# Slots of whole 256-byte lines, and pools that begin at 0 modulo 256, in a two-layer decoder kernel

## The chip, the cores and the metric

The kernel runs on one core of a Trainium2 chip. The metric is the device time of one execution in microseconds (us), as the median of several runs. On-chip memory (SBUF) has 128 partitions; an address below is a byte address within a partition, the same in all 128. TensorE multiplies a stationary operand (the weights, loaded ahead of each product) with a moving operand and adds into PSUM. VectorE, ScalarE and GpSimd work element by element, and SyncE issues most transfers.

## The reference

Two post-norm decoder layers on x (512 tokens x 1024), conditioned by a vector c. In outline, for each layer:

```
ada = silu(c) @ w_ada + b_ada                  # six rows: sh1 sc1 g1 sh2 sc2 g2
u   = layer_norm(x) * (1 + sc1) + sh1
proj = u @ w_in + b_in                         # 1024 -> 6660 columns
y_n = pooling, gated convolution, block-sparse attention, forgetting attention   # 256 wide each
merged = sum_n sigmoid(gate_n) * (y_n @ w_branch[n])
x = layer_norm(ALPHA * x + g1 * (merged @ w_o)) * ln1_g + ln1_b
u2 = layer_norm(x) * (1 + sc2) + sh2
hdn = square(relu(u2 @ w_up + b_up))           # 1024 -> 4096
x = layer_norm(ALPHA * x + g2 * (hdn @ w_down)) * ln2_g + ln2_b
```

All inputs and the output are float32.

## The kernel before

Every large product is made of three products on operands split in two: a value is rounded to the format `float32r` (the high part), and the remainder is the low part. `split` (L120 to L122) does this with one copy on ScalarE and one subtraction on VectorE; `mm3` (L126 to L129) multiplies high by high, high by low and low by high, which the trace shows as the lines L127, L128 and L129 (L85 where the first projection's order is written out by hand).

SBUF is given out by pools, one after another: `cp` (constants and small columns), `up` (25 slots of 4096 bytes called `unit`), `wp` (`uT`, and the weight buffers), `tp` (5 scratch slots called `t2`), `sp` (small columns). Within a pool, tiles of one tag share the tag's slots in turn, and a slot is as large as the largest tile of its tag. The tags of `wp` that matter here:

- `uT`, one tile: the modulated and transposed activations, 8 blocks k x (high, low) x 512 tokens, 32768 bytes.
- `whl`, 4 slots: split weights. Most tiles have 8192 bytes, as (high, low) x 8 x 128 or as 2 x 1024; `token_values` has tiles of 8 x 256 and, once in a layer, of 8 x 260 floats, 8320 bytes, which sets the size of the slots.
- `raw`, 2 slots: weights as they are loaded, with the same largest tile of 8320 bytes.
- `aw`, `rawb`, `whb`: 2048 bytes a slot.

A `t2` tile has at most 528 floats, 2112 bytes.

The work goes in stages: the first projection with its normalisation (order written by hand in `START`), `token_values`, the mixers' projections (`project`), the gates (`gates`), attention run between the tiles of other stages, the output projection (`out_project` on `w_o`), the up projection (`project` on `w_up`), and the down projection (`out_project` on `w_down`); then the second layer. In `project` a 1 MB piece of weights goes into `raw`, is split into two `whl` tiles of 128 columns, and each `whl` tile is the stationary operand of 8 k x 3 = 24 matmuls whose moving operand is a 512-token row of `uT` (for the first four tiles of two of the projections of a layer, the two 256-token halves apart). In `out_project` the activations in a `unit` slot are the stationary operand, and the weights in `whl` move: 4 token blocks x 2 halves x 3 = 24 matmuls for each k. The last k's there have their split weights in `unit` slots (`held`). In `gates`, `whl` is the stationary operand against `uT`, and `whb` against `unit`.

Waits between engines are put in by the framework from the tiles' use; the order on each engine is that of the program apart from what its planner moves.

Of the kernel before, what the change touches and what calls it, by code (L numbers as in the profile page):

```python
# [7 lines left out]
F32 = mybir.dt.float32  # L8
F32R = mybir.dt.float32r
BF16 = mybir.dt.bfloat16  # L10
# [6 lines left out]
P = 128  # L17
# [14 lines left out]
RAW_BUFS = 2  # L32
WHL_BUFS = 4
WHB_BUFS = 2
AW_BUFS = 2
T2_BUFS = 5
NH = 4
ATT_RATE = 1.1
ATT_RATE2 = 1.2
# [27 lines left out]
def decoder_kernel(ctx, tc, x, c, positions, w_ada, b_ada, w_in, b_in, w_pool, pool_scale, conv_w,  # L67
# [22 lines left out]
    cp = ctx.enter_context(tc.tile_pool(name="cp", bufs=1))  # L90
    up = ctx.enter_context(tc.tile_pool(name="up", bufs=UNITS))
    wp = ctx.enter_context(tc.tile_pool(name="wp", bufs=1))
    tp = ctx.enter_context(tc.tile_pool(name="tp", bufs=T2_BUFS))
    sp = ctx.enter_context(tc.tile_pool(name="sp", bufs=6))
    pp = ctx.enter_context(tc.tile_pool(name="pp", bufs=1, space=PSUM))

    cnt = [0]

    def nm(s):
        cnt[0] += 1  # L100
        return f"{s}_{cnt[0]}"

    def unit(shape=(P, 1024), dt=F32):
        return up.tile(list(shape), dt, tag="unit", name=nm("unit"))

    def t2(n=512, dt=F32):
        return tp.tile([P, n], dt, tag="t2", name=nm("t2"))

    def small(n=1, tag="s1"):
        return sp.tile([P, n], F32, tag=tag, name=nm("s"))  # L110
# [20 lines left out]
    def load(dst, src):  # L131

        ins = nc.sync.dma_start(dst, src)
        if ordered[0]:
            tc.keep_in_program_order(ins)
            ordered[1] = ins.ins.name
        else:
            tc.add_manual_dep(ins.ins, ordered[1], mybir.DependencyInfo(
                mybir.DependencyClass.NoSync, mybir.DependencyReason.DATA), reason="after the start")
        return ins  # L140
# [10 lines left out]
    c8 = cp.tile([KD, P], F32, name="c8")  # L151
    cst = cp.tile([P, NKEPT], F32, name="cst")
    cst2 = t2()[:, 0:NCONST - NKEPT]
    S.dma_start(c8, c[0].rearrange("(r p) -> r p", p=P))
    S.dma_start(cst, consts[:, 0:NKEPT])
    S.dma_start(cst2, consts[:, NKEPT:NCONST])
    posi = t2(dt=I32)
    G.dma_start(posi, positions.broadcast_to([P, T]))
    ident = cst[:, C_IDENT:C_IDENT + P]
# [16 lines left out]
    def mean_rstd(xt, sums):  # L176

        nmean, rstd = small(), small()
        if len(sums) == 2:
            V.tensor_scalar(nmean, sums[0], sums[1], -1.0 / D, op0=ALU.add, op1=ALU.mult)  # L180
        else:
            V.tensor_scalar(nmean, sums[0], -1.0 / D, None, op0=ALU.mult)
        S.activation(t2(1024, BF16), xt, AF.Square, bias=nmean, accum_out=rstd)  # L183
        return nmean, rstd
# [174 lines left out]
    def ada_flush():  # L359
        while pending:  # L360
            ada_step()
# [72 lines left out]
            split(uT[:, 4 * h:4 * h + 4, 0, i * P:(i + 1) * P], uT[:, 4 * h:4 * h + 4, 1, i * P:(i + 1) * P], v)  # L434


    def load_raw(shape, parts, tag="raw"):
        raw = wp.tile([P] + list(shape), F32, tag=tag, name=nm(tag), bufs=RAW_BUFS)
        for dst, src in parts:
            last_load[0] = load(dst(raw), src)  # L440
        return raw
# [1 line left out]
    last_load = [None]  # L443

    def whl(shape):
        return wp.tile([P] + list(shape), F32R, tag="whl", name=nm("whl"), bufs=WHL_BUFS)

    def kcols(w, c0, n):
        return w[:, c0:c0 + n].rearrange("(k p) m -> p k m", p=P)
# [1 line left out]
    def col_weights(w, c0, n=256):  # L451

        raw = load_raw((KD, n), [(lambda r: r, kcols(w, c0, n))])
        for j in range(n // P):
            t = whl((2, KD, P))
            split(t[:, 0], t[:, 1], raw[:, :, j * P:(j + 1) * P])
            yield t

    def project(w, tiles, evac, nh):

        heads = []
        for ci, c0 in enumerate(tiles):
            for j, t in enumerate(col_weights(w, c0)):
                idx = 2 * ci + j
                if idx < nh:
                    ps = bank("mm" if idx < PB["mm"] else "br")
                    for k in range(KD):
                        mm3(ps[:, 0:256], t[:, 0, k], t[:, 1, k], uT[:, k, 0, 0:256], uT[:, k, 1, 0:256],
                            k == 0, k == KD - 1)
                    heads.append((idx, ps, t))  # L470
                    if len(heads) == nh:
                        for i2, p2, tt in heads:
                            for k in range(KD):
                                mm3(p2[:, 256:512], tt[:, 0, k], tt[:, 1, k], uT[:, k, 0, 256:512],
                                    uT[:, k, 1, 256:512], k == 0, k == KD - 1)
                            evac(i2, p2)
                else:
                    ps = bank("mm")
                    for k in range(KD):
                        mm3(ps, t[:, 0, k], t[:, 1, k], uT[:, k, 0], uT[:, k, 1], k == 0, k == KD - 1)  # L480
                    evac(idx, ps)
                if idx >= nh + 1:
                    flush_stores()
                soon_step()
                ada_step(ada_rate[0])
                between_step(ATT_RATE)
# [4 lines left out]
    def token_values(l, c0, n):  # L491

        w = w_in[l]
        vb = sp.tile([P, 260], F32, tag="vb", name=nm("vb"), bufs=2)
        load(vb[:, :n], b_in[l:l + 1, c0:c0 + n].broadcast_to([P, n]))
        raw = load_raw((KD, n), [(lambda r: r, kcols(w, c0, n))])
        th, tl = whl((KD, n)), whl((KD, n))
        split(th, tl, raw)
        v2 = [unit((P, 2, 2, 4, 64), F32R) for _ in range(2)]
        z = None  # L500
        if n > 256:
            z = small(16, "z")
        for i in range(NT):
            ps = bank("mm")
            cs = slice(i * P, (i + 1) * P)
            for k in range(KD):
                mm3(ps[:, :n], uT[:, k, 0, cs], uT[:, k, 1, cs], th[:, k], tl[:, k], k == 0, k == KD - 1)
            vt = t2()
            V.tensor_tensor(vt[:, :n], ps[:, :n], vb[:, :n], op=ALU.add)
            v4 = vt[:, 0:256].rearrange("p (r h d) -> p r h d", r=2, h=2)  # L510
            dst = v2[i // 2][:, i % 2]
            split(dst[:, :, 0::3], dst[:, :, 1:3], v4)
            between_step(V_RATE)
            if z is not None:
                V.tensor_copy(z[:, 4 * i:4 * i + 4], vt[:, 256:260])
        return v2, z
# [192 lines left out]
    def out_project(w, grow, nk, n_outer, act, finish, g_row, b_row, xsrc):  # L709
# [13 lines left out]
        for k in range(nk):  # L723
            if k % 2 == 0:
                raw = load_raw((2, 1024), [(lambda r: r, w[k * P:(k + 2) * P, :].rearrange("(a p) m -> p a m", p=P))])
            if k < n_outer + HELD_WHL:
                t = whl((2, 1024))
                wh, wl = t[:, 0], t[:, 1]
            else:
                wh, wl = unit(dt=F32R), unit(dt=F32R)  # L730
            V.tensor_tensor(raw[:, k % 2], raw[:, k % 2], grow, op=ALU.mult)  # L731
            split(wh, wl, raw[:, k % 2])
            ah, al = act(k)
            if k < n_outer:
                for i in range(NT):
                    block(k, i, ah, al, wh, wl)
            else:
                held.append((k, ah, al, wh, wl))
            if k == nk - 2:
                with tc.issue_after(last_load[0].ins):  # L740
                    rows += [bcast(g_row), bcast(b_row)]
                    xts = [unit() for _ in range(NT)]
                    for i in range(NT):
                        load(xts[i], xsrc[i * P:(i + 1) * P, :])
# [144 lines left out]
    for l in range(DEPTH):  # L889
# [72 lines left out]
        else:  # L962
            project(w_in[l], [1024, 1280, 1792], first_evac, NH)
        wpool = [unit((P, 2, P)), unit((P, 2, 2, P), F32R)]
# [171 lines left out]
        ada_rate[0] = ADA_UP  # L1136
        project(w_up[l], list(range(0, FF, 256)), up_evac, NH)
        ada_flush()
# [68 lines left out]
```

## Time and profile before

| | us |
|---|---|
| median of 3 runs | 1622.05 |
| the 3 runs | 1623.7, 1620.67, 1622.05 |
| profiled execution, its own time | 1626.41 |
| its span, first to last instruction | 1624.6 |
| TensorE busy with matmuls | 1584.3 (98%) |
| VectorE busy | 994.4 (61%) |
| ScalarE busy | 740.4 (46%) |
[...]

The views are of the one profiled execution. [...]

### The profile page before, as it was taken

The numbers are of one execution on the slowest core, as the hardware profiler recorded it, in microseconds if no ns is written. First come the engines' busy times: TensorE is split into PE (matmuls) and PEld (weight loads), VectorE is DVE, ScalarE is ACT, GpSimd is POOL, SyncE is SP. The second block draws the span as 40 slices with busy tenths as digits, with TensorE's granted clock in tenths as the row PEclk, the third lists the DMA queues.
The fourth block names the chain that finished last, engine by engine and source line by source line (L and its number), as shares of the span: only waits on it lengthen the run. The fifth ranks groups of instructions, "written<-read, shape, count | busy, mean of one in ns | idle before, by whom it ended". The sixth has DMA issues, their size and how long they took to land.

```text
span 1624.6 us, 19880 instructions
## 1 busy us (share of the span) xinstructions
PE 1584.3 (98%) x7615; PEld 1309.9 (81%) x7615; DVE 994.4 (61%) x1641; ACT 740.4 (46%) x1230; POOL 54.8 (3%) x162
## 2 busy tenths in 40 slices
PE   5999999999999999999999999999999999999998
PEld 4878888888888888888898888778888988888886
DVE  6797455787674446744678845677467632275454
ACT  4565465443374435412365553645335543353131
POOL 1000000000010000000010000000001000000000
PEclk9999999999999999999999999999999999999999
DMA  9634223553636554332633422354216443223241
GB/s 317 185 97 154 94 88 98 168 157 117 225 101 191 187 153 134 104 104 80 244 110 120 127 75 91 117 158 153 88 62 234 147 124 95 87 104 104 79 181 52
DMA packets 151298, 215.54 MB, mean 133 GB/s; under 512 B 7564, under 2 KB 112991, under 8 KB 151203
## 3 DMA queue, kind: packets, MB, share of 16 engines
q1 hardware_dynamic: 148723, 206.84, 40.0%
q0 software_dynamic: 2176, 7.14, 1.2%
q8 instruction: 60, 0.98, 0.2%
q14 instruction: 35, 0.29, 0.1%
q10 hardware_dynamic: 304, 0.28, 0.1%
HBM read 205.33 MB, written 8.91 MB: 132 GB/s over the span
## 4 chain that ended last, share of the span: by engine, by line
PE 63%; issue 21%; DVE 8%; DMA 3%; ACT 3%; POOL 1%; SPq 1%; POOLq 0%; DVEq 0%; ACTq 0%
PE ps_mm L129 15%; PE ps_mm L127 14%; PE ps_mm L128 14%; PE ps_br L128 2%; PE ps_br L127 2%; PE ps_br L129 2%; PE ps_S L127 2%; PE ps_S L129 2%; PE ps_S L128 2%; PE ps_tr L129 2%; PE ps_tr L128 2%; PE ps_tr L127 2%; DMA aw<-in_w_ada_dram 1%; DVE whl L122 1%; DVE unit L122 1%
## 5 line engine op out<-in xcount | busy, mean ns | idle before, releaser
L127 PE MATMUL ps_mm<-uT,whl 128*128 128x512 f32 (+1 forms) x1280 | 491.6, 384 | 0.0
L129 PE MATMUL ps_mm<-uT,whl 128*128 128x512 f32 (+1 forms) x1280 | 488.7, 382 | 0.3 <-DVE whl L122 0.3
L128 PE MATMUL ps_mm<-uT,whl 128*128 128x512 f32 (+1 forms) x1280 | 487.4, 381 | 0.0
L122 DVE TENSOR_TENSOR whl<-raw,whl 128x1024 fp32r<-128x1024 f32 (+1 forms) x218 | 269.7, 1240 | 244.7 <-ACT whl L121 239.5
L121 ACT CAST whl<-raw 128x1024 fp32r<-128x1024 f32 (+1 forms) x218 | 230.0, 1059 | 193.6 <-PE ps_br L129 149.6
L129 PEld LDWEIGHTS ps_mm<-uT,whl 128*128 128x128 f32 x1280 | 241.6, 189 | 48.1 <-DVE whl L122 0.8
L128 PEld LDWEIGHTS ps_mm<-uT,whl 128*128 128x128 f32 x1280 | 241.8, 189 | 45.4
L127 PEld LDWEIGHTS ps_mm<-uT,whl 128*128 128x128 f32 x1280 | 241.7, 189 | 44.3
L317 DVE SCALAR_TENSOR_TENSOR unit<-aw,scol,unit 128x512 f32<-128x512 f32 x148 | 110.8, 748 | 99.2 <-DMA aw<-in_w_ada_dram 98.1
L1133 ACT ACTIVATE t<-ps_mm,cols 128x512 f32<-128x512 f32 x62 | 42.7, 689 | 185.8 <-PE ps_mm L129 185.8
L1078 ACT ACTIVATE t<-ps_mm,hgate 128x512 f32<-128x512 f32 x64 | 44.1, 690 | 181.3 <-PE ps_mm L129 181.1
L731 DVE TENSOR_TENSOR raw<-raw,unit 128x1024 f32<-128x1024 f32 x80 | 94.6, 1218 | 13.6 <-DMA raw<-in_w_down_dram 7.8
L1086 DVE SCALAR_TENSOR_TENSOR t<-t,ps_br 128x512 f32<-128x512 f32 x48 | 32.9, 686 | 83.9 <-PE ps_br L129 80.4
L127 PE MATMUL ps_mm<-whl,unit 128*128 128x512 f32 x180 | 70.7, 392 | 0.0
L129 PE MATMUL ps_mm<-whl,unit 128*128 128x512 f32 x180 | 70.7, 392 | 0.0
L128 PE MATMUL ps_mm<-whl,unit 128*128 128x512 f32 x180 | 70.5, 392 | 0.0
L121 ACT CAST unit<-unit 128x512 fp32r<-128x512 f32 (+1 forms) x94 | 54.5, 612 | 24.4 <-DVE unit L122 22.7
L122 DVE TENSOR_TENSOR unit<-unit,unit 128x512 fp32r<-128x512 f32 (+1 forms) x94 | 61.3, 678 | 5.8 <-ACT unit L121 5.5
L183 ACT ACTIVATE t<-unit,s 128x1024 bf16<-128x1024 f32 x28 | 32.1, 1148 | 57.0 <-DVE s L180 51.2
L188 POOL TENSOR_TENSOR s<-s,mhalf 128x1 f32<-128x1 f32 x30 | 17.2, 575 | 1026.7 <-DVE s L187 1022.1
L129 PE MATMUL ps_br<-unit,whb 128*128 128x512 f32 x128 | 50.0, 390 | 0.0
L127 PE MATMUL ps_br<-unit,whb 128*128 128x512 f32 x128 | 49.9, 390 | 0.0
(276 smaller groups left out, 2598.1 us busy)
## 6 DMA issues: line engine op xcount, KB each, us to landing
raw<-in_w_in_dram SPq DMA_DIRECT2D x47, 1024.0 KB, 5.4
aw<-in_w_ada_dram SPq DMA_DIRECT2D x160, 256.0 KB, 3.0
raw<-in_w_up_dram SPq DMA_DIRECT2D x32, 1024.0 KB, 6.0
raw<-in_w_down_dram SPq DMA_DIRECT2D x32, 1024.0 KB, 4.9
unit<-in_w_ada_dram SPq DMA_DIRECT2D x32, 256.0 KB, 5.7
rawb<-in_w_branch_dram SPq DMA_DIRECT2D x32, 256.0 KB, 3.1
raw<-in_w_o_dram SPq DMA_DIRECT2D x8, 1024.0 KB, 5.0
xmid<-unit POOLq DMA_DIRECT2D x12, 512.0 KB, 2.9
```

Of the source, the lines that this page charges most:

```text
L121: S.copy(hi, src)
L122: V.tensor_tensor(lo, src, rd(hi), op=ALU.subtract)
L127: TE.matmul(ps, wh, ah, start=first, stop=False)
L128: TE.matmul(ps, wh, al, start=False, stop=False)
L129: last_mm[0] = TE.matmul(ps, wl, ah, start=False, stop=last)
L183: S.activation(t2(1024, BF16), xt, AF.Square, bias=nmean, accum_out=rstd)
L188: G.tensor_tensor(rstd, rstd, mhalf, op=ALU.pow)
L317: V.scalar_tensor_tensor(a, aw, scol[:, k:k + 1], a, op0=ALU.mult, op1=ALU.add)
L731: V.tensor_tensor(raw[:, k % 2], raw[:, k % 2], grow, op=ALU.mult)
L1078: S.activation(tg, ps, AF.Tanh, bias=hgate[l][:, n * KD + d:n * KD + d + 1], scale=0.5)
L1086: V.scalar_tensor_tensor(tg, tg, 1.0, bp, op0=ALU.add, op1=ALU.mult)
L1133: S.activation(r, ps, AF.Relu, bias=cl[:, B_UP + idx:B_UP + idx + 1])
```

## The change

Three things about addresses, and nothing about what is computed or in which order it is written:

- `raw` and `whl` tiles are taken from a slot of `W_SLOT` = 2112 floats, 8448 bytes, which is 33 lines of 256 (before: 8320 bytes, 32.5 lines); `rawb`, which goes through the same function, from 512 floats, its size before. The function `slot` takes the whole slot and hands out its first part in the shape asked for.
- `t2` tiles are taken from slots of `T2_SLOT` = 2304 bytes, 9 lines (before: 2112 bytes, 8.25 lines).
- A tile of 40 floats, 160 bytes, that nothing reads or writes, is put first into the pool `cp`. The pools after it move up by these 160 bytes and then begin at 0 modulo 256.

```diff
+T2_SLOT = 2304
+W_SLOT = 2112
+CP_PAD = 40
...
     sp = ctx.enter_context(tc.tile_pool(name="sp", bufs=6))
+    cp.tile([P, CP_PAD], F32, name="pad")
...
     def t2(n=512, dt=F32):
-        return tp.tile([P, n], dt, tag="t2", name=nm("t2"))
+        bytes_ = 2 if dt == BF16 else 4
+        return tp.tile([P, T2_SLOT // bytes_], dt, tag="t2", name=nm("t2"))[:, 0:n]
...
+    def slot(shape, dt, tag, bufs):
+
+        n, size = 1, (W_SLOT if tag in ("raw", "whl") else 512)
+        for d in shape:
+            n *= d
+        t = wp.tile([P, size], dt, tag=tag, name=nm(tag), bufs=bufs)[:, 0:n]
+        if len(shape) == 2:
+            return t.rearrange("p (a b) -> p a b", b=shape[1])
+        return t.rearrange("p (a b c) -> p a b c", b=shape[1], c=shape[2])
+
     def load_raw(shape, parts, tag="raw"):
-        raw = wp.tile([P] + list(shape), F32, tag=tag, name=nm(tag), bufs=RAW_BUFS)
+        raw = slot(shape, F32, tag, RAW_BUFS)
...
     def whl(shape):
-        return wp.tile([P] + list(shape), F32R, tag="whl", name=nm("whl"), bufs=WHL_BUFS)
+        return slot(shape, F32R, "whl", WHL_BUFS)
```

## Rows read from the trace of the kernel before

**Rows 1.** The page: TensorE's busy time, and its granted clock in 40 slices.
```profile
PE 1584.3 (98%) x7615; PEld 1309.9 (81%) x7615; DVE 994.4 (61%) x1641; ACT 740.4 (46%) x1230; POOL 54.8 (3%) x162
...
PEclk9999999999999999999999999999999999999999
```

**Rows 2.** Busy time by stretch: us of the stretch, each engine, clock, DMA share, GB/s.
```profile
0.00:100.00 100.00, 77.26 (x386) 63.58 (x387) 78.91 (x169) 56.40 (x82) 9.48 (x25) 0.98 0.69 210
700.00:800.00 100.00, 100.00 (x437) 81.68 (x436) 47.33 (x44) 26.14 (x28) 0.00 (x0) 1.00 0.42 147
1000.00:1100.00 100.00, 95.65 (x468) 78.54 (x467) 66.27 (x140) 54.79 (x105) 2.63 (x14) 0.97 0.45 138
```

**Rows 3.** TensorE's waits: us in all, times, longest.
```profile
PE ps_tr L85 <- DVE unit L85: 7.3, 3, 4.1
...
PE ps_mm L129 <- DVE whl L122: 0.3, 1, 0.3
```

**Rows 4.** Matmuls by line and shape: count, busy us, mean ns of one.
```profile
L127 PE MATMUL ps_mm<-uT,whl 128*128 128x512 f32 x1136 | 450.8, 397 | 0.0
...
L127 PE MATMUL ps_mm<-whl,unit 128*128 128x512 f32 x180 | 70.7, 392 | 0.0
...
L127 PE MATMUL ps_tr<-whl,unit 128*128 128x512 f32 x120 | 47.1, 392 | 0.0
...
L127 PE MATMUL ps_S<-whl,unit 128*128 128x512 f32 x120 | 47.0, 392 | 0.0
...
L578 PE MATMUL ps_tr<-cst,t 128*128 128x128 f32 x160 | 28.5, 277 | 0.2
...
L127 PE MATMUL ps_mm<-uT,whl 128*128 128x256 f32 x144 | 40.9, 284 | 0.0
...
L127 PE MATMUL ps_br<-whl,unit 128*128 128x512 f32 x60 | 23.4, 390 | 0.0
```

**Rows 5.** Timeline, up projection: start us, length; every 24th start, two between.
```profile
594.73 0.40 PE L127 MATMUL ps_mm<-uT,whl 128*128 128x512 f32 x1
...
600.32 0.39 PE L127 MATMUL ps_mm<-uT,whl 128*128 128x512 f32 x1
...
601.46 0.39 PE L129 MATMUL ps_mm<-uT,whl 128*128 128x512 f32 x1
...
602.82 0.39 PE L129 MATMUL ps_mm<-uT,whl 128*128 128x512 f32 x1
...
605.78 0.40 PE L127 MATMUL ps_mm<-uT,whl 128*128 128x512 f32 x1
...
611.37 0.39 PE L127 MATMUL ps_mm<-uT,whl 128*128 128x512 f32 x1
```

**Rows 6.** Timeline, down projection: every 24th start.
```profile
673.18 0.40 PE L127 MATMUL ps_tr<-whl,unit 128*128 128x512 f32 x1
...
678.78 0.39 PE L127 MATMUL ps_tr<-whl,unit 128*128 128x512 f32 x1
...
684.23 0.40 PE L127 MATMUL ps_tr<-whl,unit 128*128 128x512 f32 x1
```

**Rows 7.** Timeline, up projection's 256-token halves: every 24th start.
```profile
479.24 0.28 PE L127 MATMUL ps_mm<-uT,whl 128*128 128x256 f32 x1
...
482.08 0.28 PE L127 MATMUL ps_mm<-uT,whl 128*128 128x256 f32 x1
...
484.96 0.28 PE L127 MATMUL ps_br<-uT,whl 128*128 128x256 f32 x1
```

**Rows 8.** Timeline, products of units with units: the first start and the 64th.
```profile
794.70 0.39 PE L127 MATMUL ps_tr<-unit,unit 128*128 128x512 f32 x1
...
808.98 0.39 PE L127 MATMUL ps_mm<-unit,unit 128*128 128x512 f32 x1
```

**Rows 9.** Timeline of VectorE, up projection: the subtractions of two successive tiles.
```profile
596.59 1.23 DVE L122 TENSOR_TENSOR whl<-raw,whl 128x1024 fp32r<-128x1024 f32 x1 [2.00 <-ACT whl L121]
...
603.90 1.22 DVE L122 TENSOR_TENSOR whl<-raw,whl 128x1024 fp32r<-128x1024 f32 x1
```

## The prediction, made before the kernel was run

> **What bounds the kernel now.** I read the page first: TensorE is busy for 1584.3 of 1624.6 us and its granted clock is in the top tenth in every slice [rows 1], so only its own pace can move the time much. The stretches say where that holds: in 700:800 it is busy all the time, at clock 1.00; it lacks 22.7 us in the first 100 us and 4.4 us in 1000:1100 [rows 2]. Its waits are short: the longest kind, on VectorE at the start, is 7.3 us in all, and the products of `uT` with `whl` (L129) wait 0.3 us in all for the splits that feed them [rows 3]. A wait that ended sooner is therefore worth next to nothing; the spacing of matmul starts is worth everything, since 4,848 products of 512 columns with a `whl` operand (3 x 1136, and 3 x 480) fill most of the span [rows 4]. "Busy" and the mean of one (397 ns) don't show this spacing, because a matmul's modelled span overlaps the next one's; I took it from the starts in the timeline.
>
> That is where this case is decided. In the up projection each `whl` tile gives 24 matmuls (8 k x 3 terms), and every 24th start is listed: tiles last 5.59, 5.46 and 5.59 us, alternating [rows 5]. In `w_down`, where `whl` is the moving operand and `unit` the weights, the groups of 24 last 5.60 and 5.45 us, alternating again [rows 6]. Within a quick tile the spacing is even: from 601.46 to 602.82 are 6 steps of 226.7 ns [rows 5]. A slow tile averages 232.9 ns.
>
> Instruction, shape, clock and operand kinds are the same in both; what alternates is the slot. A `whl` slot is as large as its largest tile, 8 x 260 x 4 = 8320 bytes, which is 32.5 lines of 256, so neighbouring slots lie 128 bytes apart modulo 256. The pad of 160 bytes brings the pools to 0 modulo 256, so they began at 96: `uT`, all `unit` slots and two of the four `whl` slots lie at 96, the other two at 224. Two operands at the same offset run at 226.7 ns; operands 128 bytes apart run at 232.9 ns, whichever of the two is the odd one. The third sort of pair agrees: held products of `unit` with `unit`, both at 96, go from 794.70 to 808.98 in 63 steps of 226.7 ns [rows 8].
>
> **The change part by part.** Sums are against the profiled execution's 1626.41 us (span 1624.6 and 1.8 around it), which stands 4.4 us above the median 1622.05; I carry the difference over to the median.
>
> *`whl` slots of 8448 bytes (33 lines).* All four slots get the same offset, that of `uT` and `unit`. Products with `whl` as weights: 3,408 / 24 = 142 tiles, half of them in odd slots, 71 x (5.59 - 5.46 = 0.13) = 9.3 us. With `whl` as moving operand: 480 x 3 / 24 = 60 groups [rows 4], 30 odd, 30 x (5.60 - 5.45 = 0.15; with unrounded starts nearer 0.14) = 4.2 us. Together 13.5 us. A quick tile also pays for the change of phase after a slow one: 5.46 against 24 x 0.2267 = 5.44, and 101 quick tiles x 0.02 = 2 us at most; I take 1.
>
> *Products of 256 columns.* Here the slots act the other way: the odd-slot tile from 479.24 takes 2.84 us, the even one from 482.08 takes 2.88 [rows 7]. There are 3 x 144 matmuls of that sort on `ps_mm` [rows 4], 18 tiles, half odd; with a few on `ps_br` I count 12 x 0.04 = 0.5 us lost.
>
> *What does not pass to the end.* The first 100 us wait for loads as well, and in 1000:1100 TensorE waits for others [rows 2]; the odd tiles there (some 9 of the 101, at 0.14) save time that is then waited for: 1.3 us given back. Elsewhere VectorE is busy for about 47 of 100 us [rows 2], so splits that must come 2% sooner still do.
>
> *Pool base at 0 instead of 96.* No row has an operand pair at 0. Nearest rows: equal offset 226.7 ns, and opposite offset 232.9 ns [rows 5]. If only the difference of the offsets counts, the base is worth nothing. [...] I take 0, the nearest row, since two addresses that are both 96 bytes off a line already give one steady value in weights, moving operands and units alike.
>
> *`t2` slots of 2304 bytes.* These were 8.25 lines, at four offsets. TensorE reads them only as weights of 160 transposes (L578) [rows 4]; 160 x 6.2 ns = 1.0 us bounds that either way; 0.
>
> *`raw`, and what ScalarE, VectorE and the DMAs do.* Successive `whl` splits, into an odd and an even slot, take 1.23 and 1.22 us [rows 9]: no price. Transfers into `raw` move the same packets; TensorE doesn't wait for them in the steady stretches. In the first 100 us a 1,024-byte run that now starts on a line touches four instead of five: at most a fifth of the 22.7 us, 4.5 us; no row shows transfers by address, and the same bytes can hardly get dearer, so 0 to 4.5, taken as 0. No instruction, wait or queue entry is added or moved; the pad is never read or written.
>
> Sum: -13.5 - 1 + 0.5 + 1.3 = -12.7 us: the profiled execution comes to 1613.7, the median to **1609.4 us**.
>
> [...]
>
> **The rivals.**
> [...] Chance 0.13.
>
> *Nothing arrives.* The slots alternate for another reason (accumulation bank, tile parity), or the saved time turns into waits on VectorE and DMA: 1622. For it: `raw` slots and the halves of a load alternate with the tiles. Against: the same step shows in `w_down`, where bank order differs, and TensorE's waits are too short to swallow it [rows 3]. Chance 0.09.
>
> *Both streams on the line start (slower).* One mechanism: at 0 modulo 256 weight load and moving operand reach their line borders at the same instant, and every pair runs at the slow spacing. The 101 quick tiles of rows 4 then last 5.59: 101 x 0.13 = 13.1 us, so 1635. It turns the sign once a 24-matmul tile at offset 0 takes more than 5.525 us, the mean of both. For it: opposite offsets change the pace at all, so border crossings matter. Against: at 96 both also cross their borders together and that is the quick case. Chance 0.09.
>
> **How the numbers follow.** The likeliest case, equal offsets at 226.7 to 227.4 ns, has 0.69 and by itself lies between 1605 and 1614. The no-effect case reaches 1623; the line-start case spreads from 1605 down to 1540, and a third of it lies above 1598. So 1598 to 1623 holds 0.69 + 0.08 + 0.04, about 0.8. A measurement here can tell 0.2%, 3.2 us, from no change: faster 0.82 (0.69 + 0.13), same 0.09, slower 0.09.
>
> **What would show it.** In the profile after, every 24 products of 512 columns should take 5.44 to 5.46 us, without alternation, in both projections; 256-column tiles 2.88 us; VectorE, ScalarE and DMA durations as before; the 4.4 us that 1000:1100 lacks should not shrink. [...]

## The result, and the profile after

The changed kernel takes 1602.83 us (median of 4 runs, 1600.55 to 1606.09) against 1621.36 for the kernel before beside it: ratio 0.9886, 95% interval 0.9864 to 0.9908. That is 18.5 us less (15 to 22), where 12.7 were forecast.

The two profiled spans differ by more, 1624.6 to 1598.7 us. A second profile of the kernel before, further below, has 1621.0: 3.6 us of the 25.9 differ between executions of one program, in waits and in the granted clock (mean 0.995 and 0.997). The order of the matmuls is the same in both programs, and the lengths on VectorE and ScalarE are too. The page of the kernel after, its span and the busy times:

```profile
span 1598.7 us, 19880 instructions
...
PE 1564.3 (98%) x7615; PEld 1305.3 (82%) x7615; DVE 994.5 (62%) x1641; ACT 740.3 (46%) x1230; POOL 54.3 (3%) x162
```

VectorE and ScalarE do what they did, to 0.1 us; TensorE's modelled busy time falls by 20 us. The timeline of the kernel after, every 24th matmul start (L132 is what L127 was): three starts in the up projection, three in the down projection, three in the up projection's 256-token halves.

```profile
585.11 0.39 PE L132 MATMUL ps_mm<-uT,whl 128*128 128x512 f32 x1
...
590.55 0.39 PE L132 MATMUL ps_mm<-uT,whl 128*128 128x512 f32 x1
...
595.99 0.39 PE L132 MATMUL ps_mm<-uT,whl 128*128 128x512 f32 x1
...
667.87 0.39 PE L132 MATMUL ps_tr<-whl,unit 128*128 128x512 f32 x1
...
673.31 0.39 PE L132 MATMUL ps_tr<-whl,unit 128*128 128x512 f32 x1
...
678.75 0.39 PE L132 MATMUL ps_tr<-whl,unit 128*128 128x512 f32 x1
...
465.21 0.28 PE L132 MATMUL ps_br<-uT,whl 128*128 128x256 f32 x1
...
468.09 0.28 PE L132 MATMUL ps_mm<-uT,whl 128*128 128x256 f32 x1
...
470.97 0.28 PE L132 MATMUL ps_mm<-uT,whl 128*128 128x256 f32 x1
```

The alternation of [rows 5, 6] is gone: each group of 24 lasts 5.44 us, 226.7 ns a product, in both projections. Each half tile lasts 2.88 us, as the even one of [rows 7] did.

Summed from start to start over all matmuls, leaving out those with a wait and those at the lower clock (0.50 of full speed), the streams are 14.7 us shorter (14.0 to 15.2 over the four pairs of a profile before and one after). Most of the rest, which was not in the sum of the prediction, lies in the first 70 us. The 217th matmul starts at 69.6 us before (68.1 in the second profile) and at 63.7 us after (63.7 again in its second profile). These are pieces from the stretch 40:65 in the chain of waits, first of the kernel before (its second profile), then of the kernel after; columns are start, length, what.

```profile
44.49 2.51 SPq L133
...
47.52 7.60 DMA rawb<-in_w_branch_dram
...
55.14 0.41 ACT whb L121
...
55.92 0.43 DVE unit L85
...
56.48 1.07 PE ps_tr L85 x8
57.56 3.79 PE ps_mm L85 x9
```

```profile
50.02 2.04 PE ps_mm L88 x9
52.06 0.68 PE ps_br L88 x3
52.74 1.36 PE ps_S L88 x6
54.10 0.84 PE ps_tr L88 x8
54.94 2.08 PE ps_mm L88 x9
```

Before, the chain goes through the queue of loads and a load until 55 us, and TensorE stands still for some 2 us behind it (1.7 us, and 1.9 in the first profile). After, it is TensorE's own work without a break until 59 us: this part of the first projection no longer waits for its loads.

In these two profiles more is lost than the standstill's own length, because the granted clock falls soon after it (in the first, whose standstill ends at 57.7 us, it is 0.50 of full speed from 59.3 to 62.7 us): above, nine products from 57.56 last 3.79 us, where nine after last 2.04. These are the stretches 40:60 and 60:80 of the kernel before, then 60:80 of the kernel after (its 40:60 stands in experiment 4); the last three columns are the granted clock as a share of full speed, the DMA share and GB/s.

```profile
40.00:60.00 20.00, 17.99 (x91) 14.58 (x90) 15.01 (x32) 9.31 (x13) 0.00 (x0) 0.98 0.83 250
60.00:80.00 20.00, 19.44 (x120) 17.33 (x119) 16.48 (x33) 13.08 (x22) 1.87 (x4) 0.93 0.37 113
```

```profile
60.00:80.00 20.00, 18.88 (x128) 16.94 (x127) 17.80 (x40) 15.51 (x26) 1.87 (x4) 1.00 0.43 133
```

The shares missing before, 0.02 and 0.07 of 20 us, are worth 1.8 us (an estimate from these rows), a part of the 4.4 to 5.9 us. The clock falls once more in 1000:1100 before (0.97, [rows 2]; 0.98 in the second profile) and not after (1.00 in both profiles).

### The profile page after: what moved, and what is told of

It reads as the page before. It is cut to its first block, busy times and chain, and to the rows that moved or that the text cites. A ratio compares the mean times of both kernels' runs of the same rounds, so it can differ in the third digit from the quotient of the medians.

```text
span 1598.7 us, 19880 instructions
## 1 busy us (share of the span) xinstructions
PE 1564.3 (98%) x7615; PEld 1305.3 (82%) x7615; DVE 994.5 (62%) x1641; ACT 740.3 (46%) x1230; POOL 54.3 (3%) x162
## 4 chain that ended last, share of the span: by engine, by line
PE 66%; issue 21%; DVE 7%; ACT 3%; DMA 1%; POOL 1%; SPq 0%; POOLq 0%; DVEq 0%; ACTq 0%
PE ps_mm L134 15%; PE ps_mm L133 15%; PE ps_mm L132 15%; PE ps_br L134 2%; PE ps_br L132 2%; PE ps_br L133 2%; PE ps_S L132 2%; PE ps_S L133 2%; PE ps_S L134 2%; PE ps_tr L132 2%; PE ps_tr L134 2%; PE ps_tr L133 2%; DVE whl L127 1%; PE ps_mm L88 1%; DMA raw<-in_w_in_dram 1%
## 5 line engine op out<-in xcount | busy, mean ns | idle before, releaser
L132 PE MATMUL ps_mm<-uT,whl 128*128 128x512 f32 (+1 forms) x1280 | 488.0, 381 | 0.0
L127 DVE TENSOR_TENSOR whl<-raw,whl 128x1024 fp32r<-128x1024 f32 (+1 forms) x218 | 269.7, 1240 | 233.0 <-ACT whl L126 227.9
L132 PEld LDWEIGHTS ps_mm<-uT,whl 128*128 128x128 f32 x1280 | 241.1, 188 | 42.0
L132 PE MATMUL ps_mm<-whl,unit 128*128 128x512 f32 x180 | 70.0, 389 | 0.0
L127 DVE TENSOR_TENSOR unit<-unit,unit 128x512 fp32r<-128x512 f32 (+1 forms) x94 | 61.3, 678 | 5.8 <-ACT unit L126 5.5
L188 ACT ACTIVATE t<-unit,s 128x1024 bf16<-128x1024 f32 x28 | 32.1, 1148 | 57.2 <-DVE s L185 51.4
```

Of the source, the lines that this page charges most:

```text
L127: V.tensor_tensor(lo, src, rd(hi), op=ALU.subtract)
L132: TE.matmul(ps, wh, ah, start=first, stop=False)
```

## The experiments

**Theory A:** the pace of a stream of products is set by the difference, modulo 256, of the addresses of weights and moving operand; only equal addresses give 226.7 ns; where the pools begin is of no account. **Rival B:** starting on a line is worth something by itself, in products or in transfers. **Rival S** (experiment 1): the longer waits of the profile before belong to its addresses, through slower transfers; Theory A has them as chance. Times stand against the kernel before, run on the same chip.

**1. The kernel before once more** (no edit).

> The kernel before once more, for a second profile of it. Two things made up the 25.9 us between the two profiled spans: 14.7 us of spacing inside the streams of matmuls, and 11 us in stalls, of which one of 3.7 us near 1070 us (VectorE and a transfer of w_ada behind it) and one of 2.3 us near 55 us are the largest. Theory A (difference of offsets; the stalls are chance of one execution): a second profile of the same program has the same alternation of 5.59 and 5.46 us per 24 products, but need not have these two stalls; its span is 1618 to 1622 us. Rival S (the stalls belong to the addresses of before, through slower transfers): both stalls stand again at the same place and with the same length within 0.5 us, and the span is 1624 to 1626 us.

Ratio 0.9998 (0.9987 to 1.001), span 1621.0. The wait near 1070 us was 2.6 us instead of 3.7, counted from start to start, so at least a part of it is chance, as A has it. The one near 55 us came back, 2.1 instead of 2.3, as S has it. The span is the one that A gave. A second profile alone does not tie the wait near 55 us to the addresses; experiments 2 to 4 do.

**2. Slots without the pad.**

```diff
-    cp.tile([P, CP_PAD], F32, name="pad")
```

> The changed kernel without the pad: all slots are whole lines, but uT, whl, unit, raw and t2 all begin at 96 modulo 256. Theory A (only the difference between the offsets of the two operands counts): 24 products of 512 columns take 5.44 us everywhere, as in the changed kernel, and the time is that of the changed kernel, 1601 to 1605 us, ratio to before 0.987 to 0.991. Rival B (starting on a line is worth something by itself): the streams are slower than 226.7 ns, or the first 100 us are slower by more than 1 us because transfers start off a line; ratio 0.992 to 1.000.

Ratio 0.9929 (0.9909 to 0.9949): 11.5 us less than before, and some 7 us short of the changed kernel. Every 24th start in its up projection (L131 is what L132 is in the changed kernel):

```profile
589.54 0.39 PE L131 MATMUL ps_mm<-uT,whl 128*128 128x512 f32 x1
...
594.98 0.39 PE L131 MATMUL ps_mm<-uT,whl 128*128 128x512 f32 x1
...
600.42 0.39 PE L131 MATMUL ps_mm<-uT,whl 128*128 128x512 f32 x1
```

Groups of 24 last 5.44 us, at offset 96 as at 0, so A holds for the products. The wait near 54 us is there, 2.8 us. B is right about the start. The 11.5 us (8 to 15) are some 3 less than the 14.7 of the streams; the mean granted clock of its six runs is 0.995 to 0.998 (median 0.996), that of the kernel before beside it 0.994 to 0.999 (median 0.997).

**3. The pad alone**, on the kernel before.

```diff
+    cp.tile([P, 40], F32, name="pad")
```

> The kernel before with the pad of 160 bytes alone: uT and unit at 0, whl and raw slots at 0 and 128 in turn, t2 slots at 0, 64, 128, 192. Theory A: alternation stays, 5.46 us for the slots at 0 and 5.59 us for the slots at 128; time as before, ratio 0.998 to 1.002. Rival B: the slots at 0 get quicker than 5.44 us per 24, and those at 128, which also start on a 128-byte border, get quicker than 5.59; ratio under 0.997.

Ratio 0.9963 (0.9950 to 0.9976), some 6 us less than before. Every 24th start in its up projection (L128 is what L127 was):

```profile
589.51 0.40 PE L128 MATMUL ps_mm<-uT,whl 128*128 128x512 f32 x1
...
595.10 0.39 PE L128 MATMUL ps_mm<-uT,whl 128*128 128x512 f32 x1
...
600.56 0.40 PE L128 MATMUL ps_mm<-uT,whl 128*128 128x512 f32 x1
```

The tiles alternate as before (5.59 and 5.46 us), so next to nothing of it comes from the pace of the products; the wait near 55 us is gone and the 217th matmul starts at 64.4 us. A alone does not explain this, and the two parts of the change add up: 11.5 + 6.0 = 17.5, against 18.5 for both. Some 2 of the 6 us go with the granted clock, by an estimate from the means over the runs: 0.9986 here, 0.9972 in the kernel before beside it, a difference of 0.0014 of 1620 us.

**4. What address a transfer wants.** The changed kernel with other pads; all slots stay whole lines.

```diff
-CP_PAD = 40
+CP_PAD = 72     # pools at 128 modulo 256
-CP_PAD = 40
+CP_PAD = 56     # pools at 64 modulo 256
```

> The changed kernel with a pad of 288 bytes: every slot still whole lines and all operands at the same offset, but the pools begin at 128 modulo 256. The pad's gain was seen in the first 60 us: with pools at 0 the loads of the start take 27.0, 46.1 and 84.0 ns per packet of 512, 1024 and 2048 bytes and the stretch 20:40 moves 375 GB/s, with pools at 96 they take 32.1, 50.6 and 94 ns and it moves 344. Theory D256 (a transfer pays for a first and last piece of a 256-byte line): at 128 the packets are as slow as at 96, the stretch moves 344 GB/s, and the time is that of the slots without pad, ratio about 0.993. Theory D64 (64-byte or 128-byte pieces): packets as at 0, 375 GB/s, ratio about 0.989. Both: 24 products of 512 columns take 5.44 us.

> The same with a pad of 224 bytes, pools at 64 modulo 256. Theory D256: slow packets (32 ns for 512 bytes), 344 GB/s in 20:40, ratio about 0.993. Theory D128: slow here and quick at 128. Theory D64: quick in both, 27 ns, 375 GB/s, ratio about 0.989. Products of 512 columns: 5.44 us per 24 in each case, if only the difference of offsets counts.

Ratios 0.9917 (0.9904 to 0.9931) and 0.9934 (0.9921 to 0.9947). The busy times of the stretches 20:40 and 40:60 follow; the last three columns are clock, DMA share and GB/s. First the slots without pad (pools at 96), then pools at 64, at 128, and the kernel after (pools at 0).

```profile
20.00:40.00 20.00, 18.47 (x89) 15.60 (x90) 19.08 (x34) 9.48 (x14) 0.31 (x1) 1.00 1.11 344
40.00:60.00 20.00, 17.57 (x84) 14.58 (x84) 14.78 (x30) 10.07 (x14) 0.00 (x0) 0.93 0.81 249
```

```profile
20.00:40.00 20.00, 18.43 (x90) 15.55 (x90) 19.12 (x35) 9.53 (x14) 0.31 (x1) 1.00 1.10 344
40.00:60.00 20.00, 17.32 (x82) 14.41 (x83) 14.59 (x30) 9.82 (x14) 0.00 (x0) 0.92 0.82 251
```

```profile
20.00:40.00 20.00, 18.38 (x81) 15.27 (x82) 17.91 (x34) 9.55 (x14) 0.31 (x1) 1.00 1.11 344
40.00:60.00 20.00, 18.09 (x93) 14.84 (x92) 15.31 (x32) 9.58 (x14) 0.00 (x0) 1.00 0.82 249
```

```profile
20.00:40.00 20.00, 18.65 (x91) 15.76 (x91) 18.90 (x33) 9.31 (x14) 0.31 (x1) 1.00 1.10 375
40.00:60.00 20.00, 20.00 (x100) 16.80 (x101) 18.13 (x37) 11.03 (x15) 0.00 (x0) 1.00 0.68 223
```

The engines of the DMA are full in 20:40 in each (share 1.10 or 1.11); they move 344 GB/s into pools at 64, 96 or 128 and 375 into pools at 0, 9% more, and TensorE then has no gap in 40:60 (busy 20.00 of 20 us). In 20:40 a packet of 512, 1024 or 2048 bytes takes 32.1, 50.5 and 93.9 ns at 64 and 32.8, 50.7 and 94.0 at 128, against 27.0, 46.1 and 84.0 at 0. Of the four starts tried only a whole line will do: D256. It is the rates that show this; the ratio at 128, 0.9917, lies between the two forecasts of the time. The granted clock also differs: 0.92 in 40:60 and 0.91 in 60:80 with pools at 64, 1.00 in both at 128, which is 3.4 us (an estimate from these shares) and enough for the difference between the two. In all eight profiles with pools at 0 the clock is 1.00 from 40 to 80 us; in four of the five others it falls after a standstill of 2.1 to 3.1 us, in the fifth (pools at 128, standstill 2.2 us) it does not. The sources of the loads stayed in these runs and the destinations moved, so these rows show a cost of the destination's address. The streams of products last 5.44 us per 24 at 64 and at 128 too.

**5. All whl slots opposite.**

```diff
     uT = wp.tile([P, KD, 2, T], F32R, name="uT")
+    wp.tile([P, 32], F32, name="shim")
```

(and the same filler behind the `whl` slots).

> The changed kernel with all four whl slots moved to 128 modulo 256 by a filler of 128 bytes behind uT (and another behind whl, so that everything else stays at 0). Theory A: every product with a whl operand runs at the slow pace, 24 of 512 columns take 5.58 to 5.60 us in both projections without alternation, so 202 tiles x 0.14 = 28 us more than the changed kernel: ratio to before about 1.003 to 1.008 (slots: twice the loss of before; the start keeps its gain). Rival (it is the alternation between two offsets that costs, not the opposite offset): 5.46 us or less, ratio about 0.989.

Ratio 1.0036 (1.0024 to 1.0048): with quick loads and all else as in the changed kernel, it is slower than before. Timeline of this kernel, every 24th start:

```profile
588.08 0.39 PE L132 MATMUL ps_mm<-uT,whl 128*128 128x512 f32 x1
...
593.65 0.40 PE L132 MATMUL ps_mm<-uT,whl 128*128 128x512 f32 x1
...
599.23 0.39 PE L132 MATMUL ps_mm<-uT,whl 128*128 128x512 f32 x1
...
667.36 0.40 PE L132 MATMUL ps_tr<-whl,unit 128*128 128x512 f32 x1
...
672.96 0.40 PE L132 MATMUL ps_tr<-whl,unit 128*128 128x512 f32 x1
```

5.57, 5.58 and 5.60 us without alternation: the opposite offset costs, not the change between two offsets. The loss against the changed kernel is 24 us (1.0036 - 0.9886, of 1621, give or take some 4) where 28 were expected. From start to start, without waits and at the full clock, the streams of this profile are some 27 us longer: 0.12 us for each 24 products with `uT` moving and 0.15 with `whl` moving.

**6. Other differences.** `whl` slots 32 bytes longer put the four slots at 0, 32, 64 and 96:

```diff
-        n, size = 1, (W_SLOT if tag in ("raw", "whl") else 512)
+        n, size = 1, (W_SLOT + 8 if tag == "whl" else W_SLOT if tag == "raw" else 512)
```

> The changed kernel with whl slots 32 bytes longer, so that the four slots lie at 0, 32, 64 and 96 modulo 256 while uT, unit and whb stay at 0; one profile gives the pace at four differences. Theory A in its simplest form (equal is quick, unequal is slow): 5.44 us per 24 at difference 0, 5.55 to 5.65 us at 32, 64 and 96. Theory A2 (the cost grows with the distance up to 128): 5.44, then about 5.48, 5.51 and 5.55. Rival B (line borders of 128 bytes): 0 quick and 32, 64, 96 all alike. Should one difference be quicker than 5.44, a still faster placing exists.

Every 24th start in its up projection (tiles at 64, 96 and 0) and in its down projection (at 32, 64 and 96):

```profile
587.35 0.40 PE L132 MATMUL ps_mm<-uT,whl 128*128 128x512 f32 x1
...
592.95 0.39 PE L132 MATMUL ps_mm<-uT,whl 128*128 128x512 f32 x1
...
598.56 0.40 PE L132 MATMUL ps_mm<-uT,whl 128*128 128x512 f32 x1
...
604.04 0.39 PE L132 MATMUL ps_mm<-uT,whl 128*128 128x512 f32 x1
...
671.90 0.40 PE L132 MATMUL ps_tr<-whl,unit 128*128 128x512 f32 x1
...
677.50 0.40 PE L132 MATMUL ps_tr<-whl,unit 128*128 128x512 f32 x1
...
683.01 0.40 PE L132 MATMUL ps_tr<-whl,unit 128*128 128x512 f32 x1
...
688.62 0.39 PE L132 MATMUL ps_tr<-whl,unit 128*128 128x512 f32 x1
```

5.60 and 5.61 us at 64 and 96, 5.48 at 0; as moving operand 5.60 at 32, 5.51 at 64, 5.61 at 96. The cost does not grow with the distance. This kernel and the next one ran once each (1627.06 and 1626.36 us), so only their paces are read.

Within a slot, tiles that begin 4, 8, 16 and 48 bytes in:

```diff
+        if tag == "whl":
+            o = (1, 2, 4, 12)[fine[0] % 4]
+            fine[0] += 1
+        t = t[:, o:o + n]
```

> The changed kernel with the whl tiles beginning 4, 8, 16 and 48 bytes into their slots in turn, so the differences to uT and unit are 4, 8, 16 and 48 bytes. Theory A2 (cost grows with distance): 4, 8 and 16 bytes as quick as 0, 226.7 to 228 ns, 48 about 232. Theory A1 (any inequality costs): all four at 231 to 235 ns, as 32, 64 and 96 were with uT moving (medians 233, 234, 234). Open: whether any of the four is under 226.7 ns.

Every 24th start in the up projection, tiles at 48, 4 and 8 bytes:

```profile
585.39 0.40 PE L132 MATMUL ps_mm<-uT,whl 128*128 128x512 f32 x1
...
590.99 0.39 PE L132 MATMUL ps_mm<-uT,whl 128*128 128x512 f32 x1
...
596.57 0.39 PE L132 MATMUL ps_mm<-uT,whl 128*128 128x512 f32 x1
...
602.10 0.40 PE L132 MATMUL ps_mm<-uT,whl 128*128 128x512 f32 x1
```

5.60, 5.58 and 5.53 us: even 4 bytes cost about as much as 128 (A1). With `whl` as the moving operand 4 bytes are the slowest pair of all, 5.67 and 5.71 us in this kernel's down projection. No difference tried was quicker than 5.44 for 512 columns.

**7. The changed kernel once more**, beside the two that follow (no edit).

> The changed kernel once more, beside the two that follow, and for a second profile of it. Theory A with D256 (14.7 us of spacing, 4 to 5 us of quicker loads at the start): ratio to before 0.987 to 0.990; the stretch 20:40 at 375 GB/s again; the wait near 1056 us short again (under 1.5 us) if it shrinks because of the change, or anywhere from 0.5 to 3.5 us if it is chance.

Ratio 0.9881 (0.9863 to 0.9899). 375 GB/s in 20:40 again. The wait near 1056 us was 1.6 us from start to start, and another of 1.5 us came at 1080, where the first profile of this kernel had none over 0.6: chance, not the change.

**8. `t2` and `raw` slots as before.**

```diff
-T2_SLOT = 2304
+T2_SLOT = 2112
...
-        n, size = 1, (W_SLOT if tag in ("raw", "whl") else 512)
+        n, size = 1, (W_SLOT if tag == "whl" else 2080 if tag == "raw" else 512)
```

> The changed kernel with the slots of t2 and raw as before (2112 and 8320 bytes), whl slots and pools as changed. If the whl slots and the pool base are all of it: the ratio of the changed kernel, 0.987 to 0.990, and the same spacing, 5.44 us per 24. Rival D (loads into raw also gain from starting on a line, through the waits for raw in the second layer and the gates): 1 to 3 us slower than the changed kernel.

Ratio 0.9894 (0.9875 to 0.9912), against 0.9881 (0.9863 to 0.9899) beside it. The streams are those of the changed kernel. The 2.4 us between the medians lie inside the intervals, and the profile has a wait of 2.6 us near 798 us where the profile beside it has less than 0.9; over the profiles of this document this wait lies between 0.9 or less and 2.7 us. A gain of 1 to 3 us from `raw` is not excluded by this.

**9. A quicker pair for the halves.** At 256 columns the kernel with slots at 0, 32, 64 and 96 (experiment 6) was quickest at a difference of 64 bytes (115.7 ns a product, against 119.9 at 0):

```diff
-            for j, t in enumerate(col_weights(w, c0)):
+            for j, t in enumerate(col_weights(w, c0, 256, 16 if 2 * ci < nh else 0)):
```

(the last argument, in floats, moves the `whl` tile within its slot).

> The changed kernel with the whl tiles of the 256-column halves (first four tiles of the first projection of layer 2 and of both up projections) beginning 64 bytes into their slots. The scan had 115.7 ns per product of 256 columns at a difference of 64 bytes, 119.9 at 0. 576 products x 4.2 ns = 2.4 us less than the changed kernel, ratio about 0.9870 to 0.9885; in the timeline 24 such products take 2.78 us instead of 2.88. Rival: the gain is lost in the changes between differences (a first 512-column tile after the halves starts out of step), 1 us or less.

Every 24th start in this kernel's halves:

```profile
471.03 0.28 PE L132 MATMUL ps_mm<-uT,whl 128*128 128x256 f32 x1
...
473.86 0.28 PE L132 MATMUL ps_mm<-uT,whl 128*128 128x256 f32 x1
...
476.68 0.28 PE L132 MATMUL ps_br<-uT,whl 128*128 128x256 f32 x1
```

2.83 and 2.82 us instead of 2.88, where 2.78 was expected; summed over the trace, 1.8 us. The ratio, 0.9883 (0.9865 to 0.9901), does not show it. It is no better version than the changed kernel as far as these runs can tell.

## Why the prediction was right, and where it was short

- *`whl` slots.* The cause and its size were right: 13.5 us were worked out for the products of 512 columns in the odd slots; from start to start they are some 13 us shorter (12.9 to 13.2 by pair of profiles). Experiments 2 and 5 show that it is the offset: equal at 96 is as quick as equal at 0 (5.44 us per 24), opposite is slow without any alternation (5.57 to 5.60).
- *The quick tiles' share* was put at 1 us and measured 0.9 to 2.2, by pair of profiles; the halves at 0.5 us lost, and 0.6 were.
- *Pool base and products.* Taken as 0, and 0 it is: 5.44 us per 24 with everything at 0, 64, 96 or 128. This ends the line-start case for the products, by which operands that begin on a line run quicker still. No run shows the pace from which the prediction has that case reach down to 1540 us: no stream of 512-column products tried was quicker than 5.44 us per 24, 226.7 ns a product.
- *The first 100 us.* This is the step that failed: "at most a fifth of the 22.7 us, 4.5 us; no row shows transfers by address [...] taken as 0". It is worth its upper bound or more: the 217th matmul starts 4.4 to 5.9 us sooner, and the pad alone brings 6 us (4 to 8). The value was taken from the lack of a row, though the stretch was known to be bound by loads, and "a wait that ended sooner is therefore worth next to nothing" was said of the whole kernel and fails at its start. The picture of lines touched has the direction right and not the sizes: by it a run of 512, 1024 or 2048 bytes on a line would save a third, a fifth and a ninth, and the packets take 16%, 9% and 11% less (32.1 to 27.0, 50.6 to 46.1 and 94 to 84.0 ns). Nor did the sum have a term for the granted clock, which stood in its rows as 0.98 and 0.97 [rows 2]; some 2 us of the pad's gain go with it.
- *`t2` and `raw` slots* were taken as 0. Experiment 8 shows no difference beyond its intervals, which leave a few us open.
- *What is given back* was put at 1.3 us. With the pad none was found: the start, which was to swallow part of it, was freed. Without it, 11.5 of the 14.7 us arrive (experiment 2); the intervals are too wide to tell how much was given back. The sign "the 4.4 us that 1000:1100 lacks should not shrink" could not be read: TensorE lacks 4.4 and 3.2 us there before, 1.2 and 3.3 after.
- *The rivals.* Nothing arrives: excluded by the ratio. The slower case, both on the line start: excluded, equal at 0 is the quick pair (5.44 us per 24).
- *The range.* 1602.83 us lies below the 1605 to 1614 of the likeliest case. It lies in the range because this was drawn down to 1598 for the line-start case in the products, which did not come true. So the pace was foreseen, and that the range holds the time is in part luck.

Sum of what was measured: 14.7 in the streams and, with the pad alone, 3.7 to 5.2 at the start (64.4 against 68.1 and 69.6) make 18.4 to 19.9 us; the ratio says 15 to 22.

## What to carry to other kernels

For products of 512 columns give weights and moving operand the same address modulo 256 (24 took 5.44 us here, and 5.57 to 5.60 at 128 bytes apart): slots of whole 256-byte lines do it, and one odd tile that sets a slot's size undoes it. Begin pools that are filled by a load-bound stretch on a whole line: into pools at 64, 96 or 128 the loads of the start ran at 344 GB/s instead of 375. Look at distances of starts, not at busy times: a product's length shows as 0.39 or 0.40 us at either pace, 226.7 or 232.9 ns.

## What was not expected of the hardware

- Equality of addresses matters down to 4 bytes: 24 products at a difference of 4 bytes took 5.58 us, at 0 5.44.
- A load's destination address sets its rate: packets of 1024 bytes took 46.1 ns into pools at 0 modulo 256 and 50.5 to 50.7 into pools at 64, 96 or 128.
- The pace depends on the length too: at 256 columns the equal pair is the slow one (2.88 us per 24, against 2.84 at 128 bytes and 2.82 or 2.83 at 64).
- The weights' address acts on the pace of the products: nothing but its value modulo 256 differs in experiment 5's up projection, and 24 products take 5.57 instead of 5.44 us. In what way the address acts on the pace, no run here shows.
